# One step of a hybrid streaming encoder: moving the stream sums from ScalarE to VectorE and queuing one E later

## The chip, the cores and the metric

The kernel runs on one core of one Trainium2 chip. The metric is device time in microseconds: 2664.24 us for the kernel before, the median of three runs (2663.28 to 2664.48). The engines are named as in the profile: PE (TensorE matmul), PEld (its weight loads), DVE (VectorE), ACT (ScalarE), POOL (GpSimd) and SP (SyncE, which issues most of the loads).

## The reference

The layer is computed for 256 prompt frames and for 8 running streams of 16 frames, 384 frames in all, with one set of weights:

```python
proj = u @ p['w_in']                       # pool | z | xBC | dt | gates
a_pool = pool_mixer(...)                   # branch A: windowed means
xbc = causal_conv(...)                     # x, B, C of branch B
y, h = ssd_scan(xh, dt, A, Bm, Cm, h0)     # Mamba-2 scan, h is the state
a_ssd = gated_rmsnorm(y, z, p['ssd_norm'])
merged = gates[:, :, 0] * (a_pool @ w_pool_proj) + gates[:, :, 1] * (a_ssd @ w_ssd_proj)
x = x + rmsnorm(merged @ w_out)
x = x + rmsnorm(square(relu(rmsnorm(x) @ w_up)) @ w_down)
```

In the scan, `decay = exp(cum[t] - cum[s])` below the diagonal, multiplied with `C B^T`, weighs the inputs of a chunk. The new state of a stream is its decayed old state plus a sum over its 16 frames of B times the weighted x. Those are the stream sums of this case; `new_ssm_sample` is the output they go to. The state is 8 streams x 64 heads x 64 x 128 numbers.

## The kernel before

**Split products.** Every projection in float32 precision is made of three matmuls in the reduced type: high weight by high input, high weight by low input, low weight by high input (`mm3`, lines 99 to 101). A weight unit is 128 x 1024 numbers, eight 128 x 128 blocks. SP loads it (line 64, tile `w`); ACT writes the high part (line 71, `wh`), DVE the low part (line 72, `wl`). Each of the three tiles has three buffers. So a unit's high part is written only when PE has finished the unit three before it, and a unit's load starts only when DVE has split the unit three before it. `take` keeps three units split ahead in the program's order: while unit n is used, the newest split is that of unit n + 2. `cut` holds the newest split's two instructions, and what stands under `later()` is queued behind them on its engine. A projection (`proj`) is two units, 48 matmuls of 128 x 384; after each of its halves one entry of the list `spill` is taken and queued under `later()`.

**Order.** An engine's instructions run in the order of its queue, and a waiting one holds all behind it. The order on PE is written out by hand in this stage (`last[0]`, `lump`). On the other engines a planner fills the queues: it goes by the program's order, its own durations and what `later()` and `behind()` demand, and lets a later instruction go first where an earlier one isn't ready by its reckoning.

**Banks.** Of PSUM's eight banks two are for projections (`mmtile`, tag mm) and six for everything else in this stage (`sstile`, tag ss). An allocation waits until the bank's last reader is done. The projections use their two in turn, and so do the product for the prompt's state (`t_pp`) and the streams' old state (`t_yi`).

**Stage of the scan.** It runs from about 424 us to 1300 us, over eight groups g of eight heads, in two half groups (pairs) each. A group has ten projections: B, C, four of x, four of z. Between them PE does short products. After the third x: transposes of two x tiles, of B, C times B (`trx`, `cb`, `trB`), Y of the group before (`yT`, `Y`), its old state's part (`yi`), then `state(prev, 0)`, the first four streams' sums of the group before. After the second z: the norm's broadcast sum of the group before (`finish`, `norm_bc`, lines 190 to 195: ACT makes `nh_g`, DVE `nl_g`, PE sums them in bank `bc_g`). After the fourth z: transposes of the other two x tiles, Y, and `state(prev, 1)`, the other four streams' sums. In group 0 there is no group before. After group 7 come gate projections (`gate_b`, 16 of them); the last group's two sets of sums stand after gates 3 and 5.

**Sums.** `state` (line 804) makes four 128 x 512 sums in four banks. Four entries of `spill` copy them into `sst`, a tile of 128 x 4 x 512 with one buffer; the fourth also issues the store on POOL's queue, which adds `sst` to what is in DRAM.

**E.** `eside(S, q)` (line 779) makes one half of the decay matrix of a pair: eight ACT instructions of 128 x 128 on the rows of cumulated decay (`cbc`, loaded by SP on line 633, two buffers), two Exps, and one product on DVE with the masked C B (line 796). Y on PE uses it.

Of the kernel before, what the change touches and what calls it, by code (L numbers as in the profile page):

```python
# [33 lines left out]
def build(ctx, tc, io):  # L34
    nc = tc.nc
    v, s, te, gp, sy = nc.vector, nc.scalar, nc.tensor, nc.gpsimd, nc.sync
# [17 lines left out]
    def sstile(name):  # L54
        return pss.tile([P, 512], F32, tag="ss", name=name)
# [60 lines left out]
    queue, ready, spill = [], [], []  # L116
# [230 lines left out]
    for b in range(3):  # L347
# [3 lines left out]
            out=dgl[:, b, :], in0=ident, scalar=y1, in1=dgh[:, b, :].bitcast(F32), op0=ALU.mult, op1=ALU.subtract  # L351
# [206 lines left out]
    def gate_b(i, pool, tag, hook=None):  # L558
        ps = proj([io["w_gb"][i, q] for q in range(2)], xg, f"gb{i}", hook)
        t = pool.tile([P, T], F32, tag=tag, name=f"gbt{i}")  # L560
        with later():
            v.tensor_tensor(halves(t), even_odd(ps), halves(rstd), ALU.mult)
            s.activation(t, t, AF.Sigmoid)
        gp.dma_start(gb_scr[i], t)

    with tc.tile_pool(name="phd", bufs=2, reuse_waits="tile") as pd, tc.tile_pool(
# [48 lines left out]
        def lump(fn):  # L615
            with behind(last[0]):
                last[0] = fn()
# [54 lines left out]
        def t_yT(S):  # L672
            S.Ys = []
            for q in range(2):
                Y = sstile(f"Y{S.nm}_{q}")
                i = te.transpose(Y[:, TP:T], S.D.yis[:, S.jp * 2 + q], ident)
                S.Ys.append(Y)
            return i

        def t_Y(S):  # L680
            for q, Y in enumerate(S.Ys):
                for sb, e0, c0, n in ((0, 0, 0, TP), (1, TP, P, P), (2, T, TP, P)):
                    for c in range(4):
                        i = te.matmul(
                            Y[c * 32 : c * 32 + 32, c0 : c0 + n],
                            S.xdt[:, q, sb, c * 32 : c * 32 + 32],
                            S.E[:, q * 2 + c // 2, e0 : e0 + n],
                            start=False,
                            stop=sb > 0,
                            skip_group_check=True,  # L690
                        )
            return i
# [14 lines left out]
        def prompt(D):  # L707
            lump(lambda: t_pp(D))
            pe = pd.tile([P, 512], F32, tag="pe", name=f"pe{D.g}", bufs=1)
            s.copy(pe, D.pp)  # L710
            gp.dma_start(io["new_ssm_p"][D.g], pe)
# [67 lines left out]
        def eside(S, q):  # L779
            if q == 0:  # L780
                S.E = pd.tile([P, 4, 512], F32, tag="E", name=f"E{S.nm}", bufs=1)
            for hh in (q * 2, q * 2 + 1):
                ch = S.cbcs[q][:, hh % 2]
                s.activation(S.E[:, hh, P:TP], ch[:, P:TP], AF.Exp, bias=tok[:, 9, S.h0 + hh : S.h0 + hh + 1])
                for b, e0 in enumerate((0, TP, T)):
                    s.activation(
                        S.E[:, hh, e0 : e0 + P],
                        ch[:, b * P : b * P + P],
                        AF.Relu,
                        bias=tok[:, b, S.h0 + hh : S.h0 + hh + 1],  # L790
                        scale=-1.0,
                    )
            Eq = S.E[:, q * 2 : q * 2 + 2]
            s.activation(Eq[:, :, :P], Eq[:, :, :P], AF.Exp, scale=-1.0)
            s.activation(Eq[:, :, TP:], Eq[:, :, TP:], AF.Exp, scale=-1.0)
            v.tensor_tensor(Eq, Eq, S.D.cbm.unsqueeze(1).to_broadcast([P, 2, 512]), ALU.mult)
# [7 lines left out]
        def state(D, k):  # L804
            su = []

            def t_su():
                for r in range(2):
                    for h in range(2):
                        t = slice(h * 64, h * 64 + 64)  # L810
                        su.append(sstile(f"su{D.g}_{k}_{r}_{h}"))
                        i = te.matmul(su[-1], D.bs[t, 2 * k + r, :], D.xst[t, 2 * k + r, :], start=True, stop=True)
                return i

            lump(t_su)
            sst = pd.tile([P, 4, 512], F32, tag="sst", name=f"sst{D.g}_{k}", bufs=1)

            def out(i):
                s.copy(sst[:, i], su[i])
                if i == 3:  # L820
                    gp.dma_start(io["new_ssm_s"][D.g, :, 4 * k : 4 * k + 4], sst, accum_op=ALU.add)

            spill.extend([lambda i=i: out(i) for i in range(4)])

        def final(S):
            D, g = S.D, S.g
# [20 lines left out]
        def finish(D):  # L847
            bc = norm_bc(pd, D.ssum, 512, f"g{D.g}", last[0])
            for j in range(4):
                i = D.g * 4 + j  # L850
                z = D.zs[j]
                v.scalar_tensor_tensor(
                    out=z, in0=z, scalar=vec[:, V_NRM + i : V_NRM + i + 1], in1=bc, op0=ALU.mult, op1=ALU.mult
                )
                gp.dma_start(a_scr[i], z)

        def pair(D, jp):
            S = Pair()
            S.D, S.g, S.jp, S.js = D, D.g, jp, (jp * 2, jp * 2 + 1)
            S.nm, S.qd = f"{D.g}_{jp}", D.g * 2 + jp  # L860
            S.h0 = S.qd * 4
            return S
# [10 lines left out]
        for g in range(G + 1):  # L873
            if g == G:
                eside(prev.p[1], 0)
                eside(prev.p[1], 1)
                for i in range(4):
                    gate_b(i, pd, "cacc")
                prompt(prev)
                lump(lambda: t_yT(prev.p[1]))  # L880
                lump(lambda: t_Y(prev.p[1]))
                state(prev, 0)
                final(prev.p[1])
                for i in range(4, 6):
                    gate_b(i, pd, "cacc")
                state(prev, 1)
                for i in range(6, 8):
                    gate_b(i, pd, "cacc")
                finish(prev)
                break  # L890
            u0 = 17 + g * 10
            D = Pair()
            D.g = g
            D.p = [pair(D, jp) for jp in range(2)]
            D.xs, D.zs = [], []
            D.BT = conv(u0, 32 + g, "BT", 1)
            pload(D)
            if g:
                eside(prev.p[1], 0)
            D.CT = conv(u0 + 1, 40 + g, "CT", 1)  # L900
            if g > 1:
                eside(prev.p[1], 1)
            D.xs.append(conv(u0 + 2, g * 4, "xs", 5))
            if g == 1:
                eside(prev.p[1], 1)
            cload(D.p[0])
            cside(D)
            D.xs.append(conv(u0 + 3, g * 4 + 1, "xs", 5))
            b2 = conv_in(u0 + 4, g * 4 + 2)
            S = D.p[0]  # L910
            if g:
                prompt(prev)
            lump(lambda: t_trx(S))
            lump(lambda: t_cb(D))
            lump(lambda: t_trB(D))
            bside(D)
            if g:
                lump(lambda: t_yT(prev.p[1]))
                lump(lambda: t_Y(prev.p[1]))
            lump(lambda: t_yi(D))  # L920
            xside(S)
            yside(D)
            mside(D)
            if g:
                state(prev, 0)
                final(prev.p[1])
            D.xs.append(taps(b2, g * 4 + 2, "xs", 5))
            D.xs.append(conv(u0 + 5, g * 4 + 3, "xs", 5))
            eside(S, 0)

            def zproj(j):
                ps = proj(in_units(u0 + 6 + j), xg, f"z{g}_{j}")
                z = pd.tile([P, T], F32, tag="zs", name=f"zs{g}_{j}", bufs=7)
                with later():
                    v.tensor_tensor(halves(z), even_odd(ps), halves(rstd), ALU.mult)
                    s.activation(z, z, AF.Silu)
                D.zs.append(z)

            zproj(0)
            eside(S, 1)  # L940
            zproj(1)
            if g:
                finish(prev)
            dside(D, 0)
            zproj(2)
            dside(D, 1)
            cload(D.p[1])
            zproj(3)
            S1 = D.p[1]
            lump(lambda: t_trx(S1))  # L950
            lump(lambda: t_yT(S))
            lump(lambda: t_Y(S))
            xside(S1)
            if g:
                state(prev, 1)
            final(S)
            stack(D)
            prev = D
# [5 lines left out]
    with ExitStack() as phe:  # L964
# [21 lines left out]
        for i in range(KD):  # L986
# [4 lines left out]
            h = mp.tile([P, T], F32R, name=f"mh{i}")  # L991
# [278 lines left out]
    with ExitStack() as mlp:  # L1270
# [218 lines left out]
        for c in range(NC - 1):  # L1489
            f, p = 8 * c + 8, 4 * c + 4  # L1490
# [206 lines left out]
```

## Time and profile before

| | before |
|---|---|
| median of three runs | 2664.24 us |
| profiled execution | 2662.44 us |
| its span, first to last instruction | 2660.7 us |
| mean granted TensorE clock | 0.993 |
| busy: PE, PEld, DVE, ACT | 2624.0, 2509.4, 1736.7, 1367.9 us |
| sums on ACT: copies, mean of one | 64, 570 ns |

A row of a timeline is: start in us, duration, engine, line, operation, what it writes <- what it reads, shape, count, and in brackets how long the engine stood idle before it and what ended that. In a view of the waits a row gives total us, times and the longest. Matmuls overlap, so their durations are longer than the steps between their starts.

### The profile page before, as it was taken

How to read it: one execution, taken by the hardware profiler on the slowest of the kernel's cores; microseconds unless marked ns; L12 is line 12 of the kernel's file. 1: busy time of each engine (PE TensorE's matmuls, PEld its weight loads, DVE VectorE, ACT ScalarE, POOL GpSimd, SP SyncE). 2: the span in 40 equal slices, each digit the busy share in tenths (PEclk: the TensorE clock that was granted, in tenths of full speed). 3: DMA queues.
4: the chain of work that ended last, by engine and by line, in shares of the span. 5: the costliest groups of instructions: out<-in, count | busy, mean ns of one | idle time of the engine just before them, and what ended most of it. 6: DMA issues, size and time to landing. Idle time of an engine off the chain costs nothing.

```text
span 2660.7 us, 39759 instructions
## 1 busy us (share of the span) xinstructions
PE 2624.0 (99%) x15761; PEld 2509.4 (94%) x15761; DVE 1736.7 (65%) x2311; ACT 1367.9 (51%) x2065; POOL 172.8 (6%) x272
## 2 busy tenths in 40 slices
PE   9999999999999999999999999999999999999998
PEld 8999999999989989999999998999999999999997
DVE  6675334777677677774644444776776868687677
ACT  5443325567667677673533333655444545454454
POOL 0000000011011011011000000000000000000000
PEclk9999999999999999999999999999999999999999
DMA  7444445766867777777754455544434344443433
GB/s 280 148 134 152 147 148 192 223 213 209 246 220 218 224 222 236 210 214 220 249 164 159 159 194 157 215 144 143 143 127 143 127 143 163 145 142 138 141 136 141
DMA packets 136475, 474.44 MB, mean 178 GB/s; under 512 B 16672, under 2 KB 35680, under 8 KB 120800
## 3 DMA queue, kind: packets, MB, share of 16 engines
q1 hardware_dynamic: 112000, 326.91, 38.6%
q0 software_dynamic: 24288, 144.99, 16.3%
q8 instruction: 124, 2.03, 0.3%
q14 instruction: 63, 0.52, 0.1%
HBM read 410.19 MB, written 61.64 MB: 177 GB/s over the span
## 4 chain that ended last, share of the span: by engine, by line
PE 94%; DVE 3%; ACT 1%; DMA 1%; issue 1%; POOL 0%; SPq 0%; DVEq 0%; ACTq 0%
PE pj_up L99 6%; PE pj_up L100 6%; PE pj_up L101 6%; PE pj_x L99 5%; PE pj_x L101 5%; PE pj_x L100 5%; PE pj_sp L100 3%; PE pj_sp L99 3%; PE pj_sp L101 3%; PE pj_z L99 2%; PE pj_z L101 2%; PE pj_z L100 2%; PE X L1408 2%; PE c L1408 2%; PE c L1406 2%; PE X L1407 2%
## 5 line engine op out<-in xcount | busy, mean ns | idle before, releaser
L99 PE MATMUL pj_up<-x1h,wh_up 128*128 128x384 f32 (+1 forms) x1024 | 333.9, 326 | 0.0
L100 PE MATMUL pj_up<-x1l,wh_up 128*128 128x384 f32 (+1 forms) x1024 | 333.7, 326 | 0.0
L101 PE MATMUL pj_up<-x1h,wl_up 128*128 128x384 f32 (+1 forms) x1024 | 333.7, 326 | 0.0
L99 PE MATMUL pj_x<-xgh,wh_x 128*128 128x384 f32 x768 | 253.6, 330 | 1.1 <-ACT wh_x L71 1.1
L101 PE MATMUL pj_x<-xgh,wl_x 128*128 128x384 f32 x768 | 251.8, 328 | 0.7 <-DVE wl_x L72 0.7
L100 PE MATMUL pj_x<-xgl,wh_x 128*128 128x384 f32 x768 | 251.6, 328 | 0.0
L71 ACT ACTIVATE wh_up<-w_up 128x1024 fp32r<-128x1024 f32 x126 | 133.1, 1057 | 190.7 <-PE pj_up L100 117.1
L100 PEld LDWEIGHTS pj_up<-x1l,wh_up 128*128 128x128 f32 x1024 | 193.5, 189 | 0.4
L99 PEld LDWEIGHTS pj_up<-x1h,wh_up 128*128 128x128 f32 x1024 | 193.5, 189 | 0.4
L101 PEld LDWEIGHTS pj_up<-x1h,wl_up 128*128 128x128 f32 x1024 | 193.5, 189 | 0.0
L72 DVE TENSOR_TENSOR wl_up<-w_up,wh_up 128x1024 fp32r<-128x1024 f32 x126 | 153.7, 1220 | 59.5 <-ACT wh_up L71 58.4
L72 DVE TENSOR_TENSOR wl_x<-w_x,wh_x 128x1024 fp32r<-128x1024 f32 x96 | 116.9, 1223 | 91.3 <-ACT wh_x L71 91.3
L101 PE MATMUL pj_z<-xgh,wl_z 128*128 128x384 f32 x512 | 170.4, 333 | 0.0
L99 PE MATMUL pj_z<-xgh,wh_z 128*128 128x384 f32 x512 | 170.2, 332 | 0.0
L100 PE MATMUL pj_z<-xgl,wh_z 128*128 128x384 f32 x512 | 169.9, 332 | 0.0
L99 PE MATMUL pj_sp<-abh,wh_sp 128*128 128x384 f32 x512 | 166.9, 326 | 0.0
L100 PE MATMUL pj_sp<-abl,wh_sp 128*128 128x384 f32 x512 | 166.9, 326 | 0.0
L101 PE MATMUL pj_sp<-abh,wl_sp 128*128 128x384 f32 x512 | 166.9, 326 | 0.0
L72 DVE TENSOR_TENSOR wl_sp<-w_sp,wh_sp 128x1024 fp32r<-128x1024 f32 x64 | 78.3, 1224 | 116.5 <-ACT wh_sp L71 116.5
L71 ACT ACTIVATE wh_sp<-w_sp 128x1024 fp32r<-128x1024 f32 x64 | 67.7, 1058 | 166.3 <-PE pj_sp L100 158.3
L99 PEld LDWEIGHTS pj_x<-xgh,wh_x 128*128 128x128 f32 x768 | 146.2, 190 | 6.4 <-issue 5.0
L101 PEld LDWEIGHTS pj_x<-xgh,wl_x 128*128 128x128 f32 x768 | 146.0, 190 | 1.0 <-DVE wl_x L72 1.0
(459 smaller groups left out, 7083.2 us busy)
## 6 DMA issues: line engine op xcount, KB each, us to landing
w_up<-w_up SPq DMA_DIRECT2D x128, 512.0 KB, 3.4
w<-w_dn POOLq DMA_DIRECT2D x60, 1024.0 KB, 5.1
w_x<-w_in SPq DMA_DIRECT2D x96, 512.0 KB, 5.2
w_z<-w_in SPq DMA_DIRECT2D x64, 512.0 KB, 4.4
w_sp<-w_ssd SPq DMA_DIRECT2D x64, 512.0 KB, 3.4
w_ga<-w_ga SPq DMA_DIRECT2D x32, 512.0 KB, 3.4
w_pp<-w_pp SPq DMA_DIRECT2D x32, 512.0 KB, 3.4
hs<-ssm POOLq DMA_DIRECT2D x16, 1024.0 KB, 8.7
```

What stands on the lines that cost most here:

```text
L71: cut[0] = s.activation(h, w, AF.Copy)
L72: cut[1] = v.tensor_tensor(l, w, h.bitcast(F32), ALU.subtract)
L99: te.matmul(out, wh, xh, start=first, stop=False, **how)
L100: te.matmul(out, wh, xl, start=False, stop=False, **how)
L101: return te.matmul(out, wl, xh, start=False, stop=last, **how)
L1406: te.matmul(o, h[:, t], vh, start=go, stop=False, skip_group_check=True)
L1407: te.matmul(o, h[:, t], vl, start=False, stop=False, skip_group_check=True)
L1408: last[0] = te.matmul(o, l[:, t], vh, start=False, stop=False, skip_group_check=True)
```

## The change

It has four edits.

- The 64 copies of stream sums go from ACT (`s.copy`) to DVE (`v.tensor_copy`). They stay in `spill`, thus under `later()`.
- In the second set of each group (k = 1) the third sum is made in a projection bank instead of one of the six others.
- The order of the copies is third, first, second, fourth (before: in order). The store still follows the fourth.
- In group 0 alone, the first pair's two `eside` calls are put under `later()`: they are queued behind the newest splits on ACT and DVE.

```diff
@@ state
-                        su.append(sstile(f"su{D.g}_{k}_{r}_{h}"))
+                        su.append((mmtile if k and (r, h) == (1, 0) else sstile)(f"su{D.g}_{k}_{r}_{h}"))
                         i = te.matmul(su[-1], D.bs[t, 2 * k + r, :], D.xst[t, 2 * k + r, :], start=True, stop=True)
...
             def out(i):
-                s.copy(sst[:, i], su[i])
+                v.tensor_copy(sst[:, i], su[i])
                 if i == 3:
                     gp.dma_start(io["new_ssm_s"][D.g, :, 4 * k : 4 * k + 4], sst, accum_op=ALU.add)
 
-            spill.extend([lambda i=i: out(i) for i in range(4)])
+            spill.extend([lambda i=i: out(i) for i in (2, 0, 1, 3)])
@@ the loop over groups
-            eside(S, 0)
+            first = nullcontext if g else later
+            with first():
+                eside(S, 0)
...
             zproj(0)
-            eside(S, 1)
+            with first():
+                eside(S, 1)
             zproj(1)
```

## The prediction

> **What bounds the kernel now.** I read the page first, then the waits of PE alone, then a table of stretches around each PE gap, then the timelines of the engine that ends each gap.
>
> ```profile
> span 2660.7 us, 39759 instructions
> PE 2624.0 (99%) x15761; PEld 2509.4 (94%) x15761; DVE 1736.7 (65%) x2311; ACT 1367.9 (51%) x2065; POOL 172.8 (6%) x272
> PE 94%; DVE 3%; ACT 1%; DMA 1%; issue 1%; POOL 0%; SPq 0%; DVEq 0%; ACTq 0%
> ```
>
> PE sets the time, and the change gives it no matmul more or less. So only gaps in PE's work can move the end. These are the gaps (total us, times, longest):
>
> ```profile
> PE bc_g L194 <- ACT nh_g L190: 9.0, 7, 1.5
> PE bc_g L195 <- DVE nl_g L191: 5.7, 7, 0.9
> PE su L812 <- DVE xdw L746: 4.8, 8, 1.6
> PE pj_gb L99 <- ACT wh_gb L71: 1.1, 1, 1.1
> PE pj_x L99 <- ACT wh_x L71: 1.1, 1, 1.1
> PE pj_x L101 <- DVE wl_x L72: 0.7, 1, 0.7
> ```
>
> They are small, but a gap costs more than its length. The table of stretches (us, PE busy, PEld, DVE, ACT, POOL, granted clock, DMA, GB/s) shows it:
>
> ```profile
> 441.85:448.10 6.25, 4.49 (x16) 3.90 (x15) 3.68 (x6) 6.22 (x13) 0.00 (x0) 0.73 0.41 129
> 450.00:463.00 13.00, 13.00 (x82) 13.00 (x81) 9.02 (x15) 11.20 (x21) 0.00 (x0) 1.00 0.52 163
> 581.55:588.08 6.53, 4.42 (x16) 3.83 (x15) 4.17 (x6) 1.68 (x5) 0.50 (x1) 0.74 1.01 300
> 965.60:968.40 2.80, 2.80 (x18) 2.80 (x19) 0.89 (x2) 0.00 (x0) 0.00 (x0) 1.00 1.02 422
> 987.60:990.50 2.90, 2.90 (x9) 2.90 (x10) 2.90 (x5) 2.88 (x6) 0.00 (x0) 0.50 0.40 136
> 556.00:583.00 27.00, 25.87 (x164) 24.00 (x156) 20.44 (x23) 25.95 (x46) 7.07 (x7) 1.00 0.73 235
> ```
>
> Undisturbed, 13.00 us hold 80 starts (82 touched, two begun earlier): 0.1625 us each. The gap in group 0 holds 14 starts, 2.28 us of work, in 6.25 us: it costs 3.97 us, though PE waits only 1.1 + 0.7. The rest is the clock, 0.73 in the mean. The norm step of group 1 costs 6.53 - 2.28 = 4.25 us in the same way. Not every gap does this: after group 5's norm step the clock stayed at 1.00 (18 matmuls in 2.80 us), and after its stream sums it was 0.50 (9 in 2.90).
>
> The Trainium skill (TensorE: Matmul & The Clock Gate, "HAM oscillation — how this bites in real kernels") gives as its abstract rule that PE must not idle longer than about 3.4 us. The trace disagrees: under 2 us of waiting brought the clock to 0.50. By the rule the group 0 gap would be worth only its 1.8 us of waiting.
>
> **Part 1: group 0's E behind the splits.** The gap at 442 us comes from E.
>
> ```profile
> 435.65 0.40 ACT L784 ACTIVATE E<-cbc,tok 128x128 f32<-128x128 f32 x1 [6.84 <-DMA cbc<-cum_scr]
> 442.18 1.04 ACT L71 ACTIVATE wh_x<-w_x 128x1024 fp32r<-128x1024 f32 x1
> 443.27 0.43 PE L99 MATMUL pj_x<-xgh,wh_x 128*128 128x384 f32 x1 [1.09 <-ACT wh_x L71]
> 444.53 0.58 PE L101 MATMUL pj_x<-xgh,wl_x 128*128 128x384 f32 x1 [0.67 <-DVE wl_x L72]
> 473.58 1.05 ACT L71 ACTIVATE wh_z<-w_z 128x1024 fp32r<-128x1024 f32 x1
> 509.39 1.94 PE L684 MATMUL Y<-E,xdt 128*32 128x256 f32 x48
> L786 ACT ACTIVATE E<-cbc,tok x192: 384/387/434, 437.7 to 1185.0; 128x128 f32<-128x128 f32 x192
> ```
>
> E's first instruction stands in ACT's queue ahead of weight splits and waits 6.84 us for the cum rows; the splits behind it are late, and PE runs dry. With the change E's first half follows the newest split in program order, two units ahead of the unit in use: the split at 473.58. Its second half follows one about 8 us later. The rows have long landed by then, and PE needs E at 509.39. Each half is 8 instructions of 0.39 us, two Exps and a table load, some 6 us on ACT. Three split units of 3.9 us (24 x 0.1625) stand ready before PE, so 6 us of ACT work is covered; if that cover were gone the splits would slip as they do now. E's two DVE products move too, into a stretch where DVE waits. The second pair of cum loads, on SP between weight loads, now waits for E to release the tiles; two more waits there could eat a few us of prefetch, no more than the present gap. Bounds: -4.0 to 0. I take **-4.0**.
>
> **Part 2: one stream sum in a projection bank.** Six sum banks, less two for the x transposes and two for Y, leave two, so the third and fourth sums of the second half (k = 1) wait until DVE has read the transposes:
>
> ```profile
> 606.05 0.47 PE L812 MATMUL su<-xst,bst 64*128 64x512 f32 x1 [0.46 <-DVE xdw L746]
> 986.17 0.46 PE L812 MATMUL su<-xst,bst 64*128 64x512 f32 x1 [1.56 <-DVE xdw L746]
> 987.10 0.50 PE L812 MATMUL su<-xst,bst 64*128 64x512 f32 x1 [0.47 <-DVE xdw L746]
> 589.80 1.06 ACT L71 ACTIVATE wh_z<-w_z 128x1024 fp32r<-128x1024 f32 x1 [6.57 <-DMA w_z<-w_in]
> ```
>
> With the third in a projection bank, the fourth needs the first transpose bank instead of the second, so the last step, 0.46 us, goes in six groups: **-2.8**. What the third waits now, the fourth then waits (group 5: 1.56 us). Bounds: 0 to -6.5 (the whole 4.8 and the slow stretch at 987.60, 9 matmuls where 18 fit, 1.5 to 1.7). The bank must be free two projections later, so the order of copies takes it first; in a full group that leaves DVE one projection (48 x 0.1625 = 7.8 us).
>
> **Part 3: 64 copies from ACT to DVE.** First the prices, from the groups of instructions:
>
> ```profile
> L819 ACT COPY sst<-su 128x512 f32<-128x512 f32 x64 | 36.5, 570 | 6.8 <-DMA new_ssm_s<-sst 6.8
> L784 ACT ACT_TABLE_LOAD x23 | 29.5, 1283 | 0.2
> L529 DVE COPY tok<-tk 128x512 f32<-128x512 f32 x1 | 0.7, 691 | 0.1
> 574.58 0.61 ACT L609 ACTIVATE xs<-cacc,vec 128x384 f32<-128x384 f32 x1
> 582.50 0.51 ACT L190 ACTIVATE nh_g<-ssum 128x384 fp32r<-128x384 f32 x1
> 583.07 0.45 PE L194 MATMUL bc_g<-nh_g,onesr 128*128 128x384 f32 x1 [1.19 <-ACT nh_g L190]
> 570.85 1.92 DVE L605 SCALAR_TENSOR_TENSOR cacc<-cbuf,vec,cacc 128x384 f32<-128x384 f32 x3
> 580.73 1.23 DVE L796 TENSOR_TENSOR E<-E,cbm 128x1024 f32<-128x1024 f32 x1 [6.07 <-ACT E L795]
> ```
>
> Ahead of the norm step ACT is the late engine: 25.95 of the 27 us before nh_g are busy, and nh_g is what PE waits for. Four copies leave that queue. The first stood where ACT waited for other work anyway, so 3 x 0.57 = 1.7 us at most come off. Against it, ACT's xs at 574.58 needs DVE's cacc, which ends at 572.77, a margin of 1.8 us. Each DVE copy ahead of it costs 0.69. With one ahead the queue gains 574.58 - 573.46 = 1.1; with two 0.4; with three it loses 0.3. After that DVE has 6.07 us idle, which hide the fourth. I take **1.0 a group**, near the case of one copy ahead, since the copies queue behind splits and DVE's state products there can also yield. The bounds are +0.3 and -3.0 (1.7 and one table load of 1.28, of which ACT does several in this stretch).
>
> I don't add the slow clock after the norm step to the gain. In group 5 it stayed away, and PE merely came earlier to the sums and waited 1.56 + 0.47 there: the DVE chain from the z weights' landing at 589.80 (or its like) to the transposes' release sets that point. It starts from the same late splits, so it moves by the 1.0 too. Seven groups: **-7.0** (+2.1 to -21.0).
>
> **A new wait at the tail.** After the last group only two projections lie between the two sets of sums:
>
> ```profile
> 1226.07 1.23 DVE L72 TENSOR_TENSOR wl_gb<-w_gb,wh_gb 128x1024 fp32r<-128x1024 f32 x1 [2.67 <-ACT wh_gb L71]
> 1226.83 0.89 POOL L821 DMA_DIRECT2D new_ssm_s<-sst  x1 [3.43 <-ACT sst L819]
> 1237.20 0.59 ACT L819 COPY sst<-su 128x512 f32<-128x512 f32 x1 [6.80 <-DMA new_ssm_s<-sst]
> 1228.93 0.74 PE L812 MATMUL su<-xst,bst 64*128 64x512 f32 x4
> 1237.51 0.33 PE L99 MATMUL pj_gb<-xgh,wh_gb 128*128 128x384 f32 x1
> new_ssm_s<-sst POOLq DMA_DIRECT2D x16, 1024.0 KB, 11.6
> ```
>
> sst has one buffer: the second set's first copy waits for the first set's store, until 1237.20. Now ACT does, and only splits stand behind it. Afterwards that copy also holds a projection bank, and gate projection 7, due at 1237.51, needs it. The store starts later too: the last copy follows the split that ends at 1227.30, so it ends near 1228.0 and POOL issues near 1228.2, 1.4 us later; it lands near 1238.6, the copy ends at 1238.6 + 0.7 = 1239.3, and PE waits 1.8 us. Behind the copy on DVE stand the next lower split and gate 6's eviction, which are needed later. 1.8 us is what group 0's gap held, so I add the same 2.2 us of slow clock: **+4.0**. Bounds: 0 (the bank goes otherwise) and +5.2 (1.2 later, at the median landing of 11.6).
>
> **Sum**: -4.0 - 2.8 - 7.0 + 4.0 = -9.8 us. The profiled execution took 2662.44 us, 1.74 more than its span; so 2652.6. The median run is 1.80 above it: **2654.4**.
>
> **Rivals.**
> *DVE takes back what ACT gives* (two or three copies ahead of cacc in every group): part 3 is 0, sum -2.8, 2661.4. For it: of the 27 us ahead of nh_g DVE is idle for 6.56, and 6.07 of them are the one wait after cacc; before it there is no room. Against: that same idle time shows that DVE's other work can be put later.
>
> *ACT gains a table load as well*: E's second half closes before xs, part 3 is 7 x -2.5 = -17.5, sum -20.3, 2643.9. For it: ACT is full there and E's pieces only fill in. Against: a queue order that no trace shows yet.
>
> *Slower: DVE becomes late at the norm step.* All four copies (2.76 us) fall ahead of cacc: it ends at 575.5, past 574.58, so nh_g and the splits before it come 1.0 us later in seven groups: +7.0. Group 5, which kept its clock, loses it: 1.5. Sum -4.0 - 2.8 + 7.0 + 1.5 + 4.0 = +5.7, 2669.9. It decides from three copies on. By the skill's rule, without slow stretches, this case would be +4.2, within the band of no change below; the rows above speak for the clock.
>
> *The first part doesn't work*: the queue order puts another waiting E ahead of a split. Sum -5.8, 2658.4, at the edge.
>
> **How the numbers follow.** Forecast 0.40, table load 0.17, DVE takes back 0.24, E still early 0.06, slower 0.13. About 0.2%, 5.3 us, is what a measurement of this kernel can tell from no change: faster is below 2658.9, slower above 2669.6. The forecast lies below with nearly all its weight, the table load wholly, E still early with half: 0.59 faster. The slower case gives 0.12. The rest, 0.29, is same. For the range I go from near the table load's end, 2642, to 2668, which leaves out the slower case and the far end of part 3.
>
> **What would show it.** Right: no pj_x wait near 442 us and clock 1.00 there; E of group 0 on ACT after 473; 1 us off the bc_g waits per group; su waits once per group, not twice; a pj_gb wait of about 2 us near the last sums, behind sst on DVE. Wrong: bc_g waits unchanged or longer with cacc or xs late; no wait at gate 7; a pause in the weight loads of group 0 behind a cum load.

## The result, and the profile after

The changed kernel takes **2628.18 us**, the median of four runs (2625.41 to 2631.03), against 2664.18 (2663.28 to 2664.48): a ratio of 0.9866, 95% interval 0.9848 to 0.9883, some 36 us less. The forecast was 2654.4 with a range down to 2642. The sign was right, the size was not. The profiled execution took 2625.41 us; its page:

```profile
span 2623.6 us, 39734 instructions
PE 2604.8 (99%) x15761; PEld 2494.5 (95%) x15761; DVE 1768.8 (67%) x2375; ACT 1306.8 (50%) x1976; POOL 160.4 (6%) x272
PE 91%; DVE 3%; issue 2%; DMA 2%; ACT 1%; POOL 0%; SPq 0%; DVEq 0%; ACTq 0%; POOLq 0%
```

PE still sets the end, with the same 15761 matmuls. DVE has 64 instructions more, the copies. ACT has 89 fewer, and the copies are only 64 of them. The other 25 are loads of its function table, as the groups of instructions on ACT show, of the kernel before first and then of the changed one (line 936 of before is line 938 of after):

```profile
L936 ACT ACT_TABLE_LOAD x14 | 18.0, 1283 | 0.2
L795 ACT ACT_TABLE_LOAD x8 | 10.3, 1283 | 0.1
L794 ACT ACT_TABLE_LOAD x8 | 10.3, 1283 | 0.1
```

```profile
L784 ACT ACT_TABLE_LOAD x19 | 24.4, 1283 | 0.3
L794 ACT ACT_TABLE_LOAD x7 | 9.0, 1283 | 0.1
L938 ACT ACT_TABLE_LOAD x2 | 2.6, 1283 | 0.0
```

With the x23 on line 784 that the prediction shows, it is 4 + 8 + 1 + 12 = 25 loads less, 25 x 1.283 = 32 us of ACT. The waits of PE after:

```profile
PE pj_p L313 <- ACT xgh L273: 2.8, 1, 2.8
PE pj_z L99 <- ACT wh_z L71: 2.3, 1, 2.3
PE su L812 <- DVE xdw L746: 1.5, 2, 0.7
PE pj_z L101 <- DVE wl_z L72: 1.5, 3, 0.9
```

The first is at the kernel's start and belongs to both kernels. Both bc_g rows, 9.0 and 5.7 us before, are gone; of the 4.8 us at the sums 1.5 are left; and there is a pj_z wait of 2.3 us that wasn't there. Landmarks on PE tell where the time went: a group transposes its x tiles twice, and between the first and the second time stand the norm step and the third and fourth z. Group 1 and the last transposes of group 7, before and then after:

```profile
551.76 0.81 PE L655 MATMUL trx<-cst,xs 128*128 128x128 f32 x6
601.89 0.82 PE L655 MATMUL trx<-cst,xs 128*128 128x128 f32 x6
...
1174.10 0.82 PE L655 MATMUL trx<-cst,xs 128*128 128x128 f32 x6
```

```profile
550.67 0.81 PE L655 MATMUL trx<-cst,xs 128*128 128x128 f32 x6
580.62 0.33 PE L194 MATMUL bc_g<-nh_g,onesr 128*128 128x384 f32 x1
597.25 0.82 PE L655 MATMUL trx<-cst,xs 128*128 128x128 f32 x6
...
1140.23 0.82 PE L655 MATMUL trx<-cst,xs 128*128 128x128 f32 x6
```

Group 1's half with the norm step took 50.13 us and takes 46.58, 3.55 less. In the same way, from such pairs of rows in all groups:

| stretch | saved, us |
|---|---|
| up to group 1's first transposes | 1.1 |
| the seven halves with a norm step: 3.55, 4.32, 4.30, 4.31, 2.76, 4.22, 2.65 | 26.1 |
| the six halves with the second sums (3.9 of it between groups 5 and 6) | 6.7 |
| from 1174.10 or 1140.23 to the end | 3.2 |
| sum, the difference of the spans | 37.1 |

So the question is how the norm step lost its whole gap. The timeline of ACT before, in the 11 us ahead of `nh_g`:

```profile
572.66 0.60 ACT L819 COPY sst<-su 128x512 f32<-128x512 f32 x1
573.29 1.28 ACT L609 ACT_TABLE_LOAD   x1
...
575.21 1.28 ACT L794 ACT_TABLE_LOAD   x1
...
576.94 1.28 ACT L936 ACT_TABLE_LOAD   x1
...
578.78 1.28 ACT L795 ACT_TABLE_LOAD   x1
...
580.61 1.99 ACT L71 ACTIVATE wh_z<-w_z 128x1024 fp32r<-128x1024 f32 x2
```

Four times in 5.5 us ACT changes its function table: Silu for `xs`, Exp for E's second half, Silu for `zs`, Exp for the rest of E. Then come the two splits of the third z and, last, `nh_g` at 582.50. The same stretch after:

```profile
566.07 1.28 ACT L794 ACT_TABLE_LOAD   x1
...
568.63 0.62 ACT L795 ACTIVATE E<-E 128x512 f32<-128x512 f32 x1
...
570.09 0.51 ACT L190 ACTIVATE nh_g<-ssum 128x384 fp32r<-128x384 f32 x1
...
573.50 1.28 ACT L609 ACT_TABLE_LOAD   x1
574.88 0.62 ACT L609 ACTIVATE xs<-cacc,vec 128x384 f32<-128x384 f32 x1
...
576.37 1.04 ACT L71 ACTIVATE wh_z<-w_z 128x1024 fp32r<-128x1024 f32 x1
```

The planner has put the rest of E ahead of the Silu. E is closed at 569.25, `nh_g` is made at 570.09, 12.4 us earlier than before, and one load is left where there were four. (The load at 566.07 has its counterpart before at 567.03. The fourth load that a group loses stood behind the norm step, at 590.87 on line 936.) PE takes `nh_g` at 580.62 without a wait. Every group from 1 to 7 looks like this.

### The profile page after: what moved, and what is told of

Read it like the earlier page. It is cut to its first block, busy times and chain, and to the rows that moved or that the text cites. A ratio compares the mean times of both kernels' runs of the same rounds, so it can differ in the third digit from the quotient of the medians.

```text
span 2623.6 us, 39734 instructions
## 1 busy us (share of the span) xinstructions
PE 2604.8 (99%) x15761; PEld 2494.5 (95%) x15761; DVE 1768.8 (67%) x2375; ACT 1306.8 (50%) x1976; POOL 160.4 (6%) x272
## 4 chain that ended last, share of the span: by engine, by line
PE 91%; DVE 3%; issue 2%; DMA 2%; ACT 1%; POOL 0%; SPq 0%; DVEq 0%; ACTq 0%; POOLq 0%
PE pj_up L99 6%; PE pj_up L100 6%; PE pj_up L101 6%; PE pj_x L99 5%; PE pj_x L100 5%; PE pj_x L101 4%; PE pj_sp L101 3%; PE pj_sp L100 3%; PE pj_sp L99 3%; PE pj_z L101 2%; PE pj_z L100 2%; PE pj_z L99 2%; PE c L1411 2%; PE X L1411 2%; PE X L1410 2%
## 5 line engine op out<-in xcount | busy, mean ns | idle before, releaser
L100 PEld LDWEIGHTS pj_x<-xgl,wh_x 128*128 128x128 f32 x768 | 145.2, 189 | 0.0
```

Source lines behind the costliest of these rows:

```text
L100: te.matmul(out, wh, xl, start=False, stop=False, **how)
```

## The experiments

The first theory, from these traces: the gain is the order of ACT's queue, above all the table loads that fell away; it hangs on the copies only because with them gone the planner closes E earlier. Its rival: the gain is the copies' own time, 0.57 us each, that left ACT. The results, each ratio against the kernel before on the same chip (its medians there lay from 2660.95 to 2663.03 us):

| kernel | median (lowest to highest), us | ratio [95%] | table loads |
|---|---|---|---|
| copies on DVE alone | 2639.50 (2624.53 to 2646.75) | 0.9908 [0.9874, 0.9942] | 55 |
| the same again | 2635.98 (2631.78 to 2640.15) | 0.9904 [0.9891, 0.9918] | 55 |
| bank and order of copies alone | 2655.89 (2652.47 to 2662.53) | 0.9984 [0.9973, 0.9995] | 83 |
| group 0's E alone | 2661.86 (2658.30 to 2666.66) | 1.0004 [0.9994, 1.0014] | 86 |
| copies and bank, no E | 2625.67 (2623.45 to 2628.98) | 0.9864 [0.9850, 0.9879] | 55 |
| the same again | 2629.77 (2624.83 to 2633.09) | 0.9880 [0.9866, 0.9894] | 55 |
| before, `nh_g` early | 2658.07 (2654.83 to 2660.09) | 0.9984 [0.9970, 0.9999] | 83 |
| whole change, copies on both engines | 2652.85 (2647.57 to 2658.46) | 0.9962 [0.9950, 0.9975] | 58 |
| before, E's second half early | 2631.33 (2630.30 to 2633.32) | 0.9878 [0.9847, 0.9909] | 55 |
| copies and bank, loads kept | 2646.72 (2643.09 to 2652.28) | 0.9948 [0.9936, 0.9960] | 83 |
| copies and bank, cum rows first | 2630.78 (2625.66 to 2631.00) | 0.9873 [0.9846, 0.9900] | 55 |
| copies and bank, E two units later | 2628.69 (2626.45 to 2631.39) | 0.9877 [0.9862, 0.9891] | 54 |
| copies and bank, E in two blocks | 2624.85 (2620.53 to 2626.55) | 0.9850 [0.9831, 0.9869] | 54 |
| the changed kernel again | 2628.24 (2627.70 to 2631.86) | 0.9864 [0.9844, 0.9884] | 58 |

**The parts alone.** Copies to DVE, nothing else:

```diff
-                s.copy(sst[:, i], su[i])
+                v.tensor_copy(sst[:, i], su[i])
```

> Only the 64 copies go to VectorE; banks, order of copies and E of group 0 as before. Theory Q (the copies' leaving ScalarE lets the planner close E's second half and the norm's high part before the conv's Silu, so the whole ScalarE queue ahead of the norm step is some 10 us earlier; this carries the gain): 83 table loads become about 55, no bc_g wait is left, time 2629 to 2636, so at least 28 of the 36 us. Theory B (the projection bank carries it, the copies are worth only their own 1.7 us a group): above 2645, bc_g waits in most groups.

Measured: 55 loads and no bc_g wait. This edit by itself changes ACT's queue. The medians are 2639.50, 3.5 us above theory Q's band but below theory B's, and 2635.98 when it was timed again. In the first timing its times spread over 22 us, more than any other kernel's; in its profiled execution, the slowest, PE waited 7.2 us at the sums and 5.4 for z splits.

The bank and the order of the copies, copies still on ACT:

```diff
-                        su.append(sstile(f"su{D.g}_{k}_{r}_{h}"))
+                        su.append((mmtile if k and (r, h) == (1, 0) else sstile)(f"su{D.g}_{k}_{r}_{h}"))
...
-            spill.extend([lambda i=i: out(i) for i in range(4)])
+            spill.extend([lambda i=i: out(i) for i in (2, 0, 1, 3)])
```

> Only the third sum's projection bank and the order of copies; the copies stay on ScalarE. Theory Q: table loads stay 83 and the seven bc_g gaps stay; at most the last su wait of a group goes, and the bank is handed back late, since ScalarE copies it late: 2659 to 2668. Theory B: below 2650.

Measured: 0.16% less, 4.3 us (1.3 to 7.2), with 83 loads and the bc_g waits about as they were (8.2 and 6.3 us). PE waits at the sums four times instead of eight, but 5.1 us in total instead of 4.8, so the trace doesn't show where the 4.3 us come from.

Group 0's E behind the splits:

```diff
-            eside(S, 0)
+            first = nullcontext if g else later
+            with first():
+                eside(S, 0)
...
-            eside(S, 1)
+            with first():
+                eside(S, 1)
```

> Only group 0's E behind the splits. My prediction's first part says -4.0: 2660. The trace after the change shows a gap of about the same size 45 us later, behind E's own table loads: by that reading the time is that of before, 2662 to 2666, with the pj_x wait gone and a pj_z wait of about 2 us in its place.

Measured: no difference that can be told (0.9994 to 1.0014), and three loads more. And the first two parts without it:

> The whole change without the edit to group 0's E. If that edit is worth nothing: 2626 to 2631 like the changed kernel, with the pj_x gap of about 4 us near 442 us back and no pj_z gap near 488. If the edit is worth the predicted 4 us: about 2632.

Measured: the whole gain, with the gap at 442 us back. The E edit gives nothing that can be told, alone or at the end.

**What in ACT's queue is it?** First, `nh_g` and `nl_g` of the kernel before are moved ahead of everything, right behind the sum of squares they read; the loads stay.

```diff
...
+            if S.jp:
+                D.hl = norm_hl(pd, D.ssum, f"g{g}")
 
         def finish(D):
-            bc = norm_bc(pd, D.ssum, 512, f"g{D.g}", last[0])
+            bc = norm_bc(pd, D.ssum, 512, f"g{D.g}", last[0], D.hl)
```

> The kernel before, with one move: the norm's high and low part are written right after the squares are summed, instead of after the second z projection; the copies stay on ScalarE, 83 table loads stay. Theory N (all that counts is that the norm's high part stands late in the queue): the bc_g gaps go, 2636 to 2641. Theory Q (the whole queue is late, the splits of the third z with it): PE passes the norm step and then waits for wh_z or wl_z of the third z instead, 1 us or more in each group; 2648 to 2660.

Measured: the bc_g waits are gone and 0.16% is won. The waits of this kernel show what stood behind them:

```profile
PE pj_z L99 <- ACT wh_z L71: 16.4, 7, 2.3
PE pj_z L101 <- DVE wl_z L72: 6.0, 7, 0.9
```

The splits of the third z, behind the four loads in the queue, now make PE wait seven times, 2.3 us each. So not `nh_g` but the queue as a whole was late.

Second, the copies stay on ACT, and in groups 1 to 7 the program emits E's second half right behind the first, before the first z:

```diff
             eside(S, 0)
+            if g:
+                eside(S, 1)
...
             zproj(0)
-            eside(S, 1)
+            if not g:
+                eside(S, 1)
```

> The kernel before with one move: in groups 1 to 7 E's second half stands right behind its first half in the program, ahead of the first z projection. The copies stay on ScalarE. The queue has 55 table loads instead of 83. Theory Q, form 1 (fewer table loads, the queue ahead of the norm step shorter): most of the gain without moving a copy, 2630 to 2645. Form 2 (the copies' own time): 2655 or more.

Measured: 31.7 us less than before in the medians, without moving one copy. `nh_g` is made 4.8 us before PE takes it, in group 1 at 575.74. Among the largest waits left after the start are these:

```profile
PE su L812 <- DVE xdw L746: 3.4, 6, 1.5
PE pj_z L101 <- DVE wl_z L72: 1.5, 7, 0.2
```

With 55 loads on ACT, copies on ACT do as well as copies on DVE (0.9878 here; 0.9908 and 0.9904 above, no bank in any of the three).

Third, the opposite: copies on DVE and the bank, but in groups 1 to 7 the last pieces of E's second half held behind the Silus, each Exp behind one:

```diff
...
-            s.activation(Eq[:, :, :P], Eq[:, :, :P], AF.Exp, scale=-1.0)
-            s.activation(Eq[:, :, TP:], Eq[:, :, TP:], AF.Exp, scale=-1.0)
+            with held(-2):
+                s.activation(Eq[:, :, :P], Eq[:, :, :P], AF.Exp, scale=-1.0)
+            with held(-1):
+                s.activation(Eq[:, :, TP:], Eq[:, :, TP:], AF.Exp, scale=-1.0)
...
```

Here `held(n)` puts an instruction behind a Silu, counted from the newest (-1); the last line-784 Exp of the half has `held(-3)` in the same way.

> Copies on DVE and the bank as in the kernel with group 0's E as before, but in groups 1 to 7 the last Exp pieces of E's second half are held behind the Silus of the last conv and of the first z, so that ACT's queue alternates between the two functions as it did before: 83 table loads instead of 55, with the copies moved all the same. Theory A (what is won is the table loads that ACT drops ahead of the third z unit's splits, 4 a group at 1.28 us): nearly all the gain goes, 2650 to 2660, with waits for the z splits in seven groups. Theory B (the copies' 0.57 us each leaving ACT is the gain): it stays, 2626 to 2635.

Measured: 2646.72, between the two theories. The 28 loads that came back, and E's second half that ends later with them, cost 17.0 us against the same kernel without them (2629.77 in the same comparison). The waits moved to splits and sums:

```profile
PE su L818 <- DVE xdw L748: 10.3, 6, 2.6
PE pj_z L101 <- DVE wl_z L72: 6.4, 8, 0.8
```

The halves tell more. In group 1 the four loads stand between 573.70 and 581 as they did before, and yet, in all, the seven halves with a norm step are 17.9 us shorter than in the kernel before (21.9 in the same kernel without the loads). With the copies gone and `nh_g` early (569.66 in group 1), PE passes the norm step without a wait although no load is missing. It is the six halves with the second sums that got worse: 9.4 us longer than before, and 6.5 shorter without the loads. DVE waits for E there just ahead of the third z's low splits, some 4.6 us in each of the seven groups (6.0 to 6.1 in the kernel before), and now it has the copies besides. In group 1:

```profile
581.21 1.23 DVE L802 TENSOR_TENSOR E<-E,cbm 128x1024 f32<-128x1024 f32 x1 [4.62 <-ACT E L801]
```

Without the loads DVE has no such wait in groups 1 to 6 and 1.9 us at most in group 7. That the sums are late for this reason is argued, not tested. So neither the loads nor the copies alone are what made the norm step late: with the loads gone and the copies kept its halves are 23.4 us shorter, with the copies gone, the bank and the loads kept 17.9. ACT's queue was late by little, 2.3 us at the splits of the third z in the run that moves only `nh_g` and `nl_g`, and either relieves it. With all loads kept the rest of the change still brings 0.52%, some 14 us. The bank (4 to 6 us) and the early `nh_g` are in that, and no run has the copies alone with the loads kept.

Fourth, the whole change with ACT making the copies too, ahead of DVE's (each sum is copied twice, so there is extra work on ACT and a longer wait on the sums' banks):

```diff
                 s.copy(sst[:, i], su[i])
+                v.tensor_copy(sst[:, i], su[i])
```

> The whole change, but ScalarE makes each copy as well, ahead of VectorE's: ScalarE has its 64 copies back and VectorE has 64 besides. The queue order stays the good one (58 table loads, the norm's high part ahead of the conv's Silu). Theory Q, form 1 (the table loads and the order carry the gain, the copies' own time hardly any): 2626 to 2638. Form 2 (the copies' own 0.57 us on ScalarE are what count): 2650 or more, with bc_g waits back.

Measured: 2652.85, some 25 us more than the changed kernel, at 58 loads. The time is that of form 2, but no bc_g wait came back. PE waits for splits of z instead (6.4 us for high parts, 9.4 for low ones) and 4.5 us at the sums; in group 1 ACT waits 8.64 us for z weights. Here DVE's copy stands behind ACT's, so both engines and the sums' banks are held longer, and what of it costs the 25 us isn't separated. It doesn't show that a copy on ACT is dear, since the kernel with E's second half early has them there at 2631.33. It is the least telling of the four.

**The bank, with the copies on DVE.**

> The same program as the run with the 64 copies on DVE alone (no bank, group 0's E as before), which gave 2639.5 us with a spread of 22 us. It is timed again beside the next kernel on the same chip, to see what the projection bank is worth once DVE makes the copies. Theory A (the bank saves one wait of about 0.5 us at the sums in each of seven groups, here as it did with the copies on ACT): 3 to 6 us above the next kernel, about 2630. Theory B (the 14 us between the two were chance in when the z weights land): within 3 us of the next kernel in the median, both with runs near 2624 and near 2640.

> Copies on DVE and one sum in a projection bank, group 0's E as before; it gave 2625.7 us. Theory A: 2625 to 2628, 3 to 6 us below the kernel without the bank. Theory B: within 3 us of it.

Measured: 2635.98 without the bank and 2629.77 with it, 6.2 us, on the same chip; 4.8 us and 2.0 us of waits at the sums. That speaks for theory A, a little past its upper end. But single runs of the two overlap, both medians lie above their forecasts, and the 2.8 us of waits are less than half of the difference.

**Group 0's gap.** Why did the E edit give nothing? The timelines of ACT and of PE after:

```profile
481.70 1.28 ACT L784 ACT_TABLE_LOAD   x1
...
483.70 1.28 ACT L938 ACT_TABLE_LOAD   x1
...
486.10 1.28 ACT L784 ACT_TABLE_LOAD   x1
...
489.41 2.94 ACT L71 ACTIVATE wh_z<-w_z 128x1024 fp32r<-128x1024 f32 x3
```

```profile
490.50 0.43 PE L99 MATMUL pj_z<-xgh,wh_z 128*128 128x384 f32 x1 [2.32 <-ACT wh_z L71]
491.95 0.43 PE L101 MATMUL pj_z<-xgh,wl_z 128*128 128x384 f32 x1 [0.86 <-DVE wl_z L72]
```

The gap moved from 442 to 490. There E's pieces stand among the Silus of the last convs and the first z, with seven loads between 469 and 487, and three splits come late in a row. One try to undo the old gap at its source was to load the first cum rows at the head of the group's program:

```diff
+            if not g:
+                cload(D.p[0])
             D.BT = conv(u0, 32 + g, "BT", 1)
...
```

> The whole change without the edit to group 0's E, but with group 0's cum rows loaded before its first projection instead of after its third. If the wait of E for these rows is the cause of the gap near 442 us, the gap goes and none comes at 488: 4 us less than the kernel without the edit, 2622 to 2626. If table loads or E's mere length make it, the gap stays and the time with it.

Measured: inconclusive. SP issued the load at 424.41, and at 425.18 and 423.99 in the two profiled executions without the edit, so it came no earlier. E still waited 6.91 us for the rows, and the gap stayed.

Another was to queue both halves of E behind the second z's splits, away from the convs:

```diff
...
             zproj(0)
-            eside(S, 1)
+            if g:
+                eside(S, 1)
             zproj(1)
+            if not g:
+                with later():
+                    eside(S, 0)
+                    eside(S, 1)
```

> The last kernel with one thing more: both halves of group 0's E are emitted behind the splits of the second z unit, so no E instruction of group 0 stands among the convs' Silus, and the queue of ACT holds 54 table loads instead of 55. Theory A (PE's gap in group 0 is made by E standing among the splits, with the cum rows' landing at 442 us and with table loads at 488 us): both gaps go, about 4 us less than the last kernel, about 2622. Rival (any 13 E instructions in a row, some 7 us of ACT with two loads, make the splits of the next z unit late wherever they stand): the gap moves to about 500 us and the time stays within 1.5 us of the last kernel.

Measured: the rival. The gap at 442 went, and another came. ACT and PE:

```profile
484.71 1.06 ACT L71 ACTIVATE wh_z<-w_z 128x1024 fp32r<-128x1024 f32 x1 [2.43 <-PE pj_z L100]
...
496.68 1.99 ACT L71 ACTIVATE wh_z<-w_z 128x1024 fp32r<-128x1024 f32 x2
```

```profile
497.77 0.43 PE L99 MATMUL pj_z<-xgh,wh_z 128*128 128x384 f32 x1 [1.24 <-ACT wh_z L71]
```

Between the two splits stand 10.9 us of E, loads and one Silu in one piece. PE frees a buffer every 3.9 us, so the next split was due at 488.6. PE wanted it at 496.5 and it takes 1.06: it could be 6.9 us late and was 8.1. What was left to try was E in two blocks with splits between them, each held behind the Silu ahead of it (`silu` holds the newest z's) so that it needs one load:

```diff
...
             zproj(0)
-            eside(S, 1)
+            with first(), behind(None if g else silu[0]):
+                eside(S, 0 if g == 0 else 1)
             zproj(1)
+            if not g:
+                with later(), behind(silu[0]):
+                    eside(S, 1)
```

> Copies on DVE and the bank, and group 0's E taken apart: the first half behind the Silu of the first z, the second half behind that of the second z, so that each half stands on ACT as one block with one table load (some 6 us) and weight splits stand between the two blocks. Theory A (group 0's gap is made by E's block or its table loads making a split later than its slack of some 9 us): no gap over 0.5 us anywhere in group 0, 54 table loads, 3 to 4 us less than the same kernel with E as before, which gave 2625.7 and 2629.8, and about as much less than the changed kernel. Rival (something else makes group 0 tight, the weight loads for one): a gap of 2 us or more is left between 430 and 510 us and the time stays within 1.5 us of the changed kernel.

> The changed kernel itself, timed beside the one before it in the list on the same chip. Its profile had its gap in group 0 at 488 us, 3.7 us in all. Theory A: 2626 to 2630, 3 to 4 us above the kernel before it in the list. Rival: within 1.5 us of it.

Measured: no gap in group 0 at all. ACT's timeline has the two blocks, each some 4.5 us long with its load, and splits behind the first:

```profile
481.21 1.28 ACT L784 ACT_TABLE_LOAD   x1
...
485.69 1.04 ACT L71 ACTIVATE wh_z<-w_z 128x1024 fp32r<-128x1024 f32 x1
...
490.44 1.28 ACT L784 ACT_TABLE_LOAD   x1
```

The median is 2624.85 us, 3.4 less than the changed kernel on the same chip and the lowest of all. The two intervals overlap, so the 3.4 us rest as much on the gap that is gone from the trace as on the times.

## Why the prediction was wrong

**Part 3, the step that failed.** The mechanism it named was right: ACT is the late engine ahead of the norm step. What failed is the sizing: "3 x 0.57 = 1.7 us at most come off", and then "**1.0 a group**". It took the order of ACT's queue from the trace of before as fixed and removed the copies from it. But the planner makes the order anew, and the loads follow from the order: a load stands wherever Exp and Silu alternate. What came off with the copies was four loads a group, three of them just ahead of `nh_g`, and `nh_g` itself came 12.4 us earlier. The halves with a norm step became 26.1 us shorter instead of 7.0. Only the bound had a load, "one table load of 1.28". The rows were there to read: four loads in 5.5 us just ahead of `nh_g`. How much of the 26.1 us is the loads' and how much the copies' stays open, since either one alone brings most of it; that the queue's order made it is shown by the run that moves only E's second half.

**The slow clock that was left out.** "I don't add the slow clock after the norm step to the gain", because the sums were to take it back. They took back nothing; the halves with the second sums became 6.7 us shorter as well. Had the step asked what is won when `nh_g` and the splits behind it are early enough, the whole gap was the answer and not a part of it: 4.25 us by its own price in group 1, and 26.1 measured over the seven halves. This is also why the lower bound of -21.0 was too high.

**The rival "ACT gains a table load as well"** named what happened: "E's second half closes before xs". It counted one load a group, 2643.9, and got a chance of 0.17. (Its -2.5 a group isn't worked out: 1.0 and one load of 1.28 make 2.3.) With the whole gap in its place it would have been -4.0 - 2.8 - 26.1 + 4.0 = -28.9, 2635.

**Part 1.** "Three split units of 3.9 us (24 x 0.1625) stand ready before PE, so 6 us of ACT work is covered" failed. Each half was not 6 us in one place: with its loads and the Silus between its pieces the queue held seven loads in 18 us. It gave 0 for -4.0. The price of the gap was about right: with E in two closed blocks the gap is gone from the trace, and the medians differ by 3.4 us.

**Part 2** was near in size: -2.8 forecast, -4.3 with copies on ACT and -6.2 with copies on DVE, at the far end of its bounds. The mechanism is borne out in part: with copies on DVE the waits at the sums fell, by 2.8 us; with copies on ACT they became fewer and no shorter in total. Two of the steps at the sums stayed after the change, 0.7 us the longest.

**The tail** was right as a mechanism, and its +4.0 is near the most that a trace shows; the changed kernel's own profile shows 0.4. POOL's queue and DVE's after:

```profile
1194.33 0.89 POOL L821 DMA_DIRECT2D new_ssm_s<-sst  x1 [4.80 <-DVE sst L819]
```

```profile
1203.22 0.69 DVE L819 COPY sst<-su 128x512 f32<-128x512 f32 x1 [5.85 <-DMA new_ssm_s<-sst]
```

The store landed 8.9 us after its issue, not after 10.4 as in the profile before; PE's steps were 0.4 us longer there. In the changed kernel's second profiled execution it took 10.3 us, and PE waited 1.53 us for the copy at full clock. In the kernel with E in two blocks it took 10.7 us, and there the foreseen wait stands in the trace, 1.92 us, with 2.1 and then 1.75 us (of slow clock) in PE's steps, 3.8 in all:

```profile
1202.96 0.40 PE L99 MATMUL pj_gb<-xgh,wh_gb 128*128 128x384 f32 x1 [1.92 <-DVE sst L819]
```

**The slower rival** had its step happen and not its effect. `cacc` did end later, since a copy and other work went ahead of it on DVE:

```profile
570.31 0.68 DVE L819 COPY sst<-su 128x512 f32<-128x512 f32 x1
...
574.24 0.60 DVE L605 SCALAR_TENSOR_TENSOR cacc<-cbuf,vec,cacc 128x384 f32<-128x384 f32 x1
```

It ends at 574.84 instead of 572.77, and `xs` waits for it. But `nh_g` no longer stands behind `xs`.

## What to carry to other kernels

Where a planner fills the queues, an edit that frees an engine also lets it choose another order; ask what the order of before costs by itself, here the table loads between two functions on the engine that is late, and price the whole gap as the upper bound of the gain. The Trainium skill (ScalarE: Activation LUTs, "Table sets: the hidden batching unit") says to group activation calls by table set; by that rule alone the edit that emits E's second half early would have been tried first, and it gave 31.7 us without touching the copies. But a load isn't a price by itself: with all 83 kept and the copies moved, most of the gain at the norm step stayed. In group 0 a block of one function on ACT cost nothing once it was shorter than what the splits behind it could wait: two blocks of 4.5 us gave no gap, one stretch of 10.9 us did.

## What the runs showed of the hardware

The clock after a gap is not set by the length of that gap alone. The changed kernel had the same gap in group 0 in both profiled executions, 2.3 and 0.9 us of waiting. The stretches around and behind it (us, PE busy, PEld, DVE, ACT, POOL, granted clock, DMA, GB/s), of the first execution and of the second:

```profile
487.86:492.60 4.74, 1.57 (x8) 0.97 (x8) 3.07 (x3) 4.72 (x10) 0.00 (x0) 1.00 0.47 188
492.60:500.60 8.00, 8.00 (x51) 8.00 (x50) 3.81 (x5) 3.72 (x5) 0.00 (x0) 1.00 0.78 249
```

```profile
491.11:495.85 4.74, 1.56 (x6) 0.97 (x6) 3.06 (x3) 4.72 (x10) 0.00 (x0) 0.86 0.45 163
495.85:501.13 5.28, 5.28 (x19) 5.28 (x18) 2.03 (x3) 1.68 (x2) 0.00 (x0) 0.50 0.84 293
```

The same program, the same wait: once at full clock, once at 0.50 over 5.28 us, 19 matmuls where the rate of the row above (51 in 8.00 us) gives 34. The half of group 0 that holds the gap took 47.1 us in the first execution and 50.1 in the second, 3 us of difference behind equal waits. Whether both ran on one chip isn't on record, and what decides the clock was not found.
